# A decoder trunk on one core: scores of the second tile moved behind the retention's outputs, norm rows through the weight queue, an earlier start of ScalarE

## The chip, the cores and the metric

The kernel runs on one core of a Trainium2 chip. The time is that of one launch on the device, in microseconds (us), and every comparison is made with the kernel before on the same chip. The engines are named as in the profile: PE (TensorE, matrix products), DVE (VectorE), ACT (ScalarE), POOL (GpSimd) and SP (SyncE, which only issues transfers here). They run their own instruction streams and meet at semaphores.

## The reference, cut to what matters

256 tokens of width 1024 pass through two layers, all in float32:

```
h += 0.5 * SwiGLU_1(RMSNorm(h))
u  = RMSNorm(h);  z = u @ W_in
h += W_o( sigmoid(gA) * (RWKV7(z_A) @ P_A) + sigmoid(gB) * (Retention(z_B) @ P_B) )
h += CrossAttn_4heads(RMSNorm(h), RMSNorm(mem))
h += 0.5 * SwiGLU_2(RMSNorm(h))
out = RMSNorm(h)                      # after the last layer
```

The retention branch forms scores of query and key tiles (128 tokens each), multiplies them with the values, normalizes each head of 128 columns and multiplies by a row `gn` and a gate:

```
y = _standardize(y, B_GN_EPS).reshape(B, T, B_V_WIDTH) * gn
return y * silu(g)
```

The RWKV-7 branch is a recurrence over tokens; the kernel computes it in two tiles of 128 tokens, in which blocks of triangular systems are inverted.

## The kernel before, in words

Each float32 operand of a product is split into a high part (`wh`, `uh`, ...: rounded, line 241, on ACT) and a low part (`wl`, `ul`, ...: the rest, line 242, on DVE), and three products are formed (high by high, high by low, low by high). Weights come in pieces of 512 KB over SP's queue (line 260) into five raw buffers; the split fills seven pairs of buffers.

PE's order of work is written out by a planner (`Em`, line 77). Each part of the network is a generator that emits its products and then yields a number, the modelled nanoseconds it wants to wait, or an event; the planner takes the ready generator of the best priority. So big projections (`z<-wh,uh` and the like, from `mix`) are interleaved with the chains of the two mixers. PE executes that order strictly. The orders of DVE, ACT, POOL and SP are chosen by a scheduler from dependencies and its own estimates, with the start (line 470) and the ends under a high priority as exceptions; each engine then executes its list strictly too.

PSUM is handed out in eight banks (`s.ps`, a first-in first-out list of free banks), so a product may have to wait until the last reader of its bank is done.

What the change touches:
- `start` (line 470): DVE clears a tile `zero`, PE multiplies it by itself 20 times, ACT makes the first `uh` and `wh`.
- `rw_chain` (line 1124). The products `sc<-beT,alT` give U; its blocks go to HBM (`ug`) and back (`us`), and POOL solves 31 steps, each a product `tm<-xs,us` (line 1162) and a sum `xs<-xs,tm` (line 1167). The result goes out as `xg` (line 1170), comes back as `W` (line 1250), is turned by DVE (`XQ<-W`, line 1254), and PE continues with `iv<-XQ,U`. Ahead of that the generator `late(t)` (line 1180) makes, for each tile t, the scores `sc<-qT,beT` and two groups `sc<-mh,kh` ..., which DVE masks into `S<-sc` (line 1121). The products `R<-zv,S` come from `r_sum(0)`, between `late(0)` and `late(1)`.
- `ret_chain` (line 1410): scores `sc<-bqT,bkT`, masked into `rS`, then four tiles `O<-bv,rS` (24 rows of products in PE's list). For each, ACT squares into `yb`, DVE sums (`bss`), POOL forms the power -1/2 (`brn<-bss,nhalf`, line 265), and DVE multiplies, `yb<-O,brn` (line 1449), which is the last reader of the O bank.
- `ret_g` (line 1398): the gate of the retention; it loads `gn` over POOL's queue and ends in `bg<-bg,rhf,gn` (line 1406) on DVE.
- `acc_last` and `final` (lines 375 and 620): the last additions to h and the final RMSNorm.

Of the kernel before, what the change touches and what calls it, by code (L numbers as in the profile page):

```python
# [10 lines left out]
F32 = mybir.dt.float32  # L11
F32R = mybir.dt.float32r
I32 = mybir.dt.int32
AF = mybir.ActivationFunctionType
ALU = mybir.AluOpType
AX = mybir.AxisListType
P = 128
D = 1024
# [143 lines left out]
class K:  # L162
    NW = 7
    NRAW = 5
    NA = 49
    T_XG, T_W = 57000.0, 6000.0

    def __init__(s, ctx, tc, A):
        s.tc, s.nc, s.A = tc, tc.nc, A
# [71 lines left out]
        s.nc.scalar.activation(hi, src, AF.Copy)  # L241
        s.nc.vector.tensor_tensor(lo, src, hi.bitcast(F32), ALU.subtract)  # L242

    def row(s, ap, name):
        t = s.ar.alloc(name)
        s.nc.gpsimd.dma_start(t, ap.partition_broadcast(P))
        return t

    def load_w(s, view, n, c):
# [18 lines left out]
    def behind(s, ins, other):  # L268

        s.tc.add_manual_dep(ins.ins, other.ins.name, mybir.DependencyInfo(  # L270
            mybir.DependencyClass.NoSync, mybir.DependencyReason.DATA), reason="behind")

    def stats(s, src, n, eps):
        nc = s.nc
        sq = s.ar.alloc("sq0"), s.ar.alloc("sq1")
        ss = s.sm.tile([P, 2], F32, name="ss", tag="ss")
        for i in range(2):
            nc.scalar.activation(sq[i], src[i], AF.Square, accum_out=ss[:, i:i + 1])
        s.ar.free(*sq)
        x = s.sm.tile([P, 1], F32, name="sx", tag="sx")  # L280
        nc.vector.tensor_tensor(x, ss[:, 0:1], ss[:, 1:2], ALU.add)
        nc.vector.tensor_scalar(x, x, 1.0 / n, eps, ALU.mult, ALU.add)
        r = s.sm.tile([P, 1], F32, name="rstd", tag="rstd")
        s.pow_(r, x, 1)
        return r


    def wcols(s, key, dram, c0, c):
# [85 lines left out]

    def acc_last(s, parts, acc, scale):

        ws = [s.W.next(key) for _, key, _ in parts]
        for t in range(2):
            tok = slice(t * P, (t + 1) * P)
            for n in range(2):  # L380
                cs = slice(n * 512, n * 512 + 512)
                for i, (X, key, k) in enumerate(parts):
                    xh, xl = (x[:, tok] for x in X(k))
                    s.mm3(acc[t][n], xh, xl, ws[i][0][:, 0, cs], ws[i][1][:, 0, cs], False, i == len(parts) - 1)
                with s.tc.high_priority():
                    s.nc.vector.scalar_tensor_tensor(s.h[t][n], acc[t][n], scale[t], s.h[t][n], ALU.mult, ALU.add)
                s.ps.free(acc[t][n])
                yield 0
            s.final(t)


    def new_u(s, l, i):
# [77 lines left out]
    def start(s):  # L470

        nc = s.nc
        with s.tc.manual_schedule(engines={nc.vector.engine, nc.scalar.engine}):

            x = s.ar.alloc("zero", F32R, (P, 256))
            nc.vector.memset(x.bitcast(F32), 0.0)
            b = s.ps.alloc("zero")
            for i in range(20):
                nc.tensor.matmul(b[:, 0:256], x[:, 0:P], x, start=i == 0, stop=i == 19)
            s.ps.free(b)  # L480
            s.ar.free(x)
            for j in range(4):
                s.prep_u(2 * j)
                s.prep_u(2 * j + 1)
                s.W.fill(j + 1)
                if j < 3:
                    nc.sync.dma_start(s.hT[:, 2 * j + 2:2 * j + 4, :], s.A["xT"][:, 2 * j + 2:2 * j + 4, :])
            nc.scalar.activation(s.gcol[:, 64:96], s.gcol[:, 64:96], AF.Copy, scale=0.5)
        for j in range(4):
            s.prep_ss(j, 11414.0, 6590.0, nc.gpsimd)  # L490
            s.ev_u[j].t = 0.0
# [125 lines left out]
        for n in range(2):  # L617
            s.nc.gpsimd.dma_start(s.gain[n], s.A["final_norm"][n * 512:(n + 1) * 512].partition_broadcast(P))

    def final(s, t):  # L620
        nc = s.nc
        with s.tc.high_priority():
            r = s.stats(s.h[t], D, 1e-6)
            o = []
            for n in range(2):
                o.append(s.ar.alloc("o"))
                nc.vector.tensor_tensor(o[n], s.h[t][n], s.gain[n], ALU.mult)
            nc.vector.tensor_scalar(o[0], o[0], r, None, ALU.mult)
            nc.scalar.activation(o[1], o[1], AF.Copy, scale=r)
            for n, q in ((0, nc.sync), (1, nc.scalar)):  # L630
                q.dma_start(s.A["out"][0, t * P:(t + 1) * P, n * 512:n * 512 + 512], o[n])
        s.ar.free(*o)


    def setup(s):
        for l in range(DEPTH):
# [79 lines left out]
    def mix(s, l):  # L716
        nc, A = s.nc, s.A
        em = s.em
        X = s.Xu

        def two():
            yield from s.psneed(2)
            return [s.ps.alloc("z"), s.ps.alloc("z")]
# [14 lines left out]
        R = s.R = {"rows": rows}  # L738
# [14 lines left out]
        for nm, q in (("bq", 0), ("bk", 1)):  # L753
            ps = yield from two()
            yield from s.unit(X, nm, 8, 512, ps)
            em.spawn(s.ret_rot(nm, q, ps), 4)
        R["bv"] = [[], []]
        for n in range(2):
            ps = yield from two()
            yield from s.unit(X, "bv", 8, 512, ps)  # L760
            s.ret_v(s.evac(ps, "bv"))
        R["ev_bv"].t = em.now + 4150.0
        em.spawn(s.ret_chain(l), 4)
        R["bg"] = [[], []]
        for n in range(2):
            ps = yield from two()
            yield from s.unit(X, "bg", 8, 512, ps)
            s.ret_g(l, n, ps)
# [52 lines left out]
        acc = [s.ps.alloc("acc") for n in range(4)]  # L821
# [302 lines left out]
    def rw_chain(s, l):  # L1124
# [8 lines left out]
        for t in range(2):  # L1133
# [6 lines left out]
            for k in range(4):  # L1140
                for q in range(2):
# [5 lines left out]
        xs = s.ar.alloc("xs", F32, (P, 16, 32))  # L1147
        tm = s.ar.alloc("tm", F32, (P, 16, 32))
        nc.gpsimd.dma_start(xs, A["x0"])
        nc.gpsimd.tensor_tensor(tm[:, 0:2, 0:29], xs[:, 0:2, 2:3].broadcast_to([P, 2, 29]),  # L1150
                                xs[:, 2:3, 3:32].broadcast_to([P, 2, 29]), ALU.mult)
        for i in range(2):
            for q in range(2):
                nc.sync.dma_start(us[i][q * 64:(q + 1) * 64], ug[:, 16 * i:16 * i + 16, :])
# [18 lines left out]
        t_sol = em.now  # L1173
# [6 lines left out]
        def late(t):  # L1180
            al, q, ka = (T[t][n] for n in ("al", "q", "ka"))
            yield from s.psneed(2)
            yield from s.arneed(2)
            b = s.scores(T[t]["be"], q)
            s.ar.free(T[t]["be"])
            for o in range(2):
                QB[t][o] = s.ar.alloc("S", F32, (P, 4, P))
                s.mask_evac(QB[t][o], b[o], s.masks[:, 1:2, :].broadcast_to([P, 4, P]))
            yield from s.arneed(6)
            kh, kl = (s.ar.alloc(n, F32R, (P, 4, P)) for n in ("kh", "kl"))  # L1190
            s.split(kh, kl, ka)
            s.ar.free(ka)
            mv = [[s.ar.alloc(n, F32R, (P, 2, 2, P)) for n in ("mh", "ml")] for _ in range(2)]
            for i in range(2):
                for c, x in enumerate((al, q)):
                    s.split(mv[i][0][:, :, c, :], mv[i][1][:, :, c, :], x[:, 2 * i:2 * i + 2, :])
            if t == 0:
                s.ar.free(al, q)
            KQ[t][:] = [], []
            for i in range(2):  # L1200
                yield 1776.0
                yield from s.psneed(2)
                yield from s.arneed(2)
                b = [s.ps.alloc("sc") for _ in range(2)]
                for pr in range(2):

                    for n, (x, y) in enumerate(((kh, 0), (kh, 1), (kl, 0))):
                        for o in range(2):
                            p0, p1 = 64 * o, 64 * o + 64
                            s.mm(b[o][:, pr * 256:pr * 256 + 256], x[p0:p1, 2 * i + pr, :],  # L1210
                                 mv[i][y][p0:p1, pr].rearrange("p c t -> p (c t)"), n == 0, n == 2)
                s.em.now -= 650.0
                for o in range(2):
                    x = s.ar.alloc("S", F32, (P, 2, 2, P))
                    s.mask_evac(x, b[o], s.masks.unsqueeze(1).broadcast_to([P, 2, 2, P]))
                    KQ[t][o].append(x)
            s.ar.free(kh, kl, *mv[0], *mv[1])
            yield 5258.0
# [7 lines left out]
        def r_sum(t):  # L1226
            vc = R["v"][t]
            b = s.ps.alloc("R")
            for hd in range(8):
                if t == 1 and hd % 2 == 0:  # L1230
                    s.mm(ps2(b, hd // 2), T[1]["al"][:, hd // 2, :], s.S0[:, hd // 2, :], True, False)
                s.mm(hs(b, hd), kq(t, hd, 0), hs(vc, hd), t == 0, t == 0 or hd % 2 == 1)
            rr = s.ar.alloc("R")
            act.activation(rr, b, AF.Copy)
            s.ps.free(b)
            return rr
# [42 lines left out]

        yield from s.psneed(1)  # L1280
        r0 = r_sum(0)
        yield from late(1)
        yield from inv()
        for t in range(2):
# [112 lines left out]

    def ret_g(s, l, n, ps):
        nc, R = s.nc, s.R
        gn = s.row(s.A["b_gn"][l, n * 512:(n + 1) * 512], "gn")  # L1400
        for t in range(2):
            th = s.ar.alloc("bg")
            nc.scalar.activation(th, ps[t], AF.Tanh, scale=s.rhf[t])
            nc.vector.scalar_tensor_tensor(th, th, 1.0, ps[t], ALU.add, ALU.mult)
            s.ps.free(ps[t])
            nc.vector.scalar_tensor_tensor(th, th, s.rhf[t], gn, ALU.mult, ALU.mult)
            R["bg"][t].append(th)
        s.ar.free(gn)
# [330 lines left out]
```

## Time and profile before

| | us |
|---|---|
| three runs | 1518.89, 1518.98, 1520.46 |
| median | 1518.98 |
| the profiled execution | 1518.1 |
| its span, first to last instruction | 1516.0 |
| PE busy in it | 1495.0 (99%) |
| DVE, ACT, POOL busy | 1061.9, 760.5, 180.7 |
| PE's mean granted clock | 0.992 of full speed |

A row of a timeline gives the start, the duration, the engine, the line, what is written from what, and in brackets how long the engine had stood idle just before and what released it. Rows of one kind that follow one another are drawn together (x16); then the duration is that of the whole group. Products overlap in PE, so the spacing of two starts is what one costs.

### The profile page before, as it was taken

What the parts mean: (1) busy time and instruction counts of PE and PEld (TensorE: products, weight loads), DVE (VectorE), ACT (ScalarE), POOL (GpSimd) and SP (SyncE); (2) the same over time, 40 slices, a digit from 0 to 9 for tenths busy, and PEclk for the clock granted to TensorE, in tenths of its full rate; (3) what the DMA queues carried; (4) which work ended last, traced back from release to release, by engine and by line L of the source; (5) the groups of instructions that cost most, each with busy time, mean ns of one, the idle gap of its engine ahead of it and who ended that gap; (6) DMA issues with size and microseconds to landing.
All of it is one profiled execution on the core that took longest, in us unless ns stands there. A gap on an engine that the chain in (4) does not pass through costs nothing.

```text
span 1516.0 us, 28626 instructions
## 1 busy us (share of the span) xinstructions
PE 1495.0 (99%) x11754; PEld 1417.9 (94%) x11754; DVE 1061.9 (70%) x1463; ACT 760.5 (50%) x1044; POOL 180.7 (12%) x241
## 2 busy tenths in 40 slices
PE   8999999998999999999999999999999999999997
PEld 8999988788999999999999999887889999999996
DVE  7976699967657757655686666899576577665654
ACT  6554465544434656444455445654454446654442
POOL 3210003272000000000001000224700000000000
PEclk9999999999999999999999999999999999999999
DMA  8776655535546545666568665674364455466651
GB/s 303 228 226 195 195 169 189 152 123 181 168 145 190 170 139 183 191 185 188 173 196 244 195 194 156 193 232 138 95 197 157 156 164 191 126 211 184 189 186 41
DMA packets 137546, 270.54 MB, mean 178 GB/s; under 512 B 18804, under 2 KB 29444, under 8 KB 137416
## 3 DMA queue, kind: packets, MB, share of 16 engines
q1 hardware_dynamic: 133960, 259.94, 55.2%
q0 software_dynamic: 3024, 8.19, 1.9%
q8 instruction: 92, 1.51, 0.4%
q10 hardware_dynamic: 432, 0.58, 0.1%
q14 instruction: 38, 0.31, 0.1%
HBM read 263.31 MB, written 2.23 MB: 175 GB/s over the span
## 4 chain that ended last, share of the span: by engine, by line
PE 83%; DVE 6%; POOL 4%; issue 2%; DMA 2%; ACT 1%; SPq 1%; POOLq 0%; DVEq 0%
PE z L207 21%; PE acc L207 21%; PE u L207 16%; PE g L207 16%; PE xq L207 3%; POOL tm L1162 2%; DVE wl L242 2%; POOL xs L1167 1%; PE tp L219 1%; PE Y L207 1%; PE xo L207 1%; PE xs L207 1%; POOL brn L265 1%; PE SA L207 1%; PE sc L207 1%
## 5 line engine op out<-in xcount | busy, mean ns | idle before, releaser
L242 DVE TENSOR_TENSOR wl<-raw,wh 128x1024 fp32r<-128x1024 f32 (+1 forms) x477 | 580.8, 1224 | 312.7 <-ACT wh L241 310.5
L241 ACT ACTIVATE wh<-raw 128x1024 fp32r<-128x1024 f32 (+1 forms) x477 | 501.2, 1057 | 527.6 <-PE z L207 125.6
L207 PE MATMUL g<-uh,wh 128*128 128x256 f32 x704 | 196.9, 280 | 2.0 <-ACT wh L241 2.0
L207 PE MATMUL g<-uh,wl 128*128 128x256 f32 x704 | 196.7, 279 | 0.9 <-DVE wl L242 0.9
L207 PE MATMUL u<-uh,wh 128*128 128x256 f32 x704 | 196.5, 279 | 0.0
L207 PE MATMUL g<-ul,wh 128*128 128x256 f32 x704 | 196.3, 279 | 0.0
L207 PE MATMUL u<-ul,wh 128*128 128x256 f32 x704 | 195.8, 278 | 0.0
L207 PE MATMUL u<-uh,wl 128*128 128x256 f32 x704 | 195.8, 278 | 0.0
L207 PE MATMUL acc<-ah,wh 128*128 128x256 f32 x528 | 146.9, 278 | 0.0
L207 PE MATMUL acc<-al,wh 128*128 128x256 f32 x528 | 146.6, 278 | 0.0
L207 PE MATMUL acc<-ah,wl 128*128 128x256 f32 x528 | 146.6, 278 | 0.0
L207 PEld LDWEIGHTS g<-uh,wh 128*128 128x128 f32 x704 | 132.9, 189 | 2.4 <-ACT wh L241 2.2
L207 PEld LDWEIGHTS g<-uh,wl 128*128 128x128 f32 x704 | 133.0, 189 | 1.3 <-DVE wl L242 1.3
L207 PEld LDWEIGHTS g<-ul,wh 128*128 128x128 f32 x704 | 132.6, 188 | 0.2
L207 PEld LDWEIGHTS u<-uh,wl 128*128 128x128 f32 x704 | 132.3, 188 | 0.0
L207 PEld LDWEIGHTS u<-uh,wh 128*128 128x128 f32 x704 | 132.2, 188 | 0.0
L207 PEld LDWEIGHTS u<-ul,wh 128*128 128x128 f32 x704 | 131.9, 187 | 0.0
L207 PE MATMUL z<-wh,uh 128*128 128x512 f32 (+1 forms) x320 | 126.6, 396 | 0.0
L207 PE MATMUL z<-wh,ul 128*128 128x512 f32 (+1 forms) x320 | 123.2, 385 | 0.4 <-DVE ul L415 0.4
L207 PE MATMUL z<-wl,uh 128*128 128x512 f32 (+1 forms) x320 | 123.3, 385 | 0.0
L207 PEld LDWEIGHTS acc<-ah,wl 128*128 128x128 f32 x528 | 99.2, 188 | 0.0
L207 PEld LDWEIGHTS acc<-ah,wh 128*128 128x128 f32 x528 | 99.1, 188 | 0.0
(404 smaller groups left out, 3311.9 us busy)
## 6 DMA issues: line engine op xcount, KB each, us to landing
raw<-in_ffn_w_in SPq DMA_DIRECT2D x175, 512.0 KB, 4.1
raw<-in_mix_w_in SPq DMA_DIRECT2D x108, 512.0 KB, 4.4
raw<-in_ffn_w_out SPq DMA_DIRECT2D x88, 512.0 KB, 3.5
raw<-in_cross_w_kv SPq DMA_DIRECT2D x32, 512.0 KB, 3.7
raw<-in_w_branch_b SPq DMA_DIRECT2D x16, 512.0 KB, 4.5
raw<-in_mix_w_out SPq DMA_DIRECT2D x16, 512.0 KB, 3.5
raw<-in_cross_w_q SPq DMA_DIRECT2D x16, 512.0 KB, 3.8
raw<-in_cross_w_o SPq DMA_DIRECT2D x16, 512.0 KB, 4.3
```

What stands on the lines that cost most here:

```text
L207: s.nc.tensor.matmul(out, l, r, start=start, stop=stop)
L219: s.nc.tensor.transpose(out, src, s.ident)
L241: s.nc.scalar.activation(hi, src, AF.Copy)
L242: s.nc.vector.tensor_tensor(lo, src, hi.bitcast(F32), ALU.subtract)
L265: i = s.nc.gpsimd.tensor_tensor(out, src, s.nhalf[:, :n], ALU.pow)
L1162: i = nc.gpsimd.tensor_tensor(tm[:, 0:nr, 0:w], xc, row, ALU.mult)
L1167: nc.gpsimd.tensor_tensor(xs[:, 0:nr, k + 1:32], xs[:, 0:nr, k + 1:32], tm[:, 0:nr, 0:w], ALU.add)
```

## The change

Seven edits:
1. ACT reads one column of `zero` right after DVE cleared it, so its table is loaded there and not when hT has landed.
2. 30 products of zeros instead of 20.
3. The rows `gn` are asked for on SP's queue, ahead of the second `bv` unit and of the first `bg` unit, instead of on POOL's queue in `ret_g`.
4. A product on POOL ahead of the solve, whose result nothing read, is gone.
5. `late(1)` waits for the modelled time t_sol + 42 us.
6. T_W, the modelled wait between `W` and `XQ`, is 7500 instead of 6000.
7. The final norm's squares are taken in `acc_last` with the scale 1/32, and the epsilon is added to the first half's sum.

```diff
-    T_XG, T_W = 57000.0, 6000.0
+    T_XG, T_W = 57000.0, 7500.0
...
-    def row(s, ap, name):
+    def row(s, ap, name, q=None):
         t = s.ar.alloc(name)
-        s.nc.gpsimd.dma_start(t, ap.partition_broadcast(P))
+        (q or s.nc.gpsimd).dma_start(t, ap.partition_broadcast(P))
...
+                    sq = s.ar.alloc("sq")
+                    nc.scalar.activation(sq[:, c0:c1], h, AF.Square, scale=1.0 / 32, accum_out=ss[:, e:e + 1])
+                    s.ar.free(sq)
+                    if e == 0:
+                        nc.vector.tensor_scalar(x, ss[:, 0:1], 1e-6, None, ALU.add)
+                    else:
+                        nc.vector.tensor_tensor(x, x, ss[:, e:e + 1], ALU.add)
...
+            nc.scalar.activation(s.sm.tile([P, 1], F32, name="act0", tag="act0"), x[:, 0:1].bitcast(F32), AF.Copy)
             b = s.ps.alloc("zero")
-            for i in range(20):
-                nc.tensor.matmul(b[:, 0:256], x[:, 0:P], x, start=i == 0, stop=i == 19)
+            for i in range(30):
+                nc.tensor.matmul(b[:, 0:256], x[:, 0:P], x, start=i == 0, stop=i == 29)
...
+        R["gn"] = []
+        gn = lambda n: R["gn"].append(s.row(A["b_gn"][l, n * 512:(n + 1) * 512], "gn", nc.sync))
         for n in range(2):
+            if n:
+                gn(0)
             ps = yield from two()
...
         for n in range(2):
+            if n == 0:
+                gn(1)
             ps = yield from two()
...
-        nc.gpsimd.tensor_tensor(tm[:, 0:2, 0:29], xs[:, 0:2, 2:3].broadcast_to([P, 2, 29]),
-                                xs[:, 2:3, 3:32].broadcast_to([P, 2, 29]), ALU.mult)
...
         r0 = r_sum(0)
+        yield max(0.0, t_sol + 42000.0 - em.now)
         yield from late(1)
...
-        gn = s.row(s.A["b_gn"][l, n * 512:(n + 1) * 512], "gn")
+        gn = R["gn"].pop(0)
```

PE's list in the first layer, from the products R on, was this before; the left-out rows are projections `z` and repetitions.

```order
L207 MATMUL R<-zv,S 128x64 x8
L207 MATMUL sc<-qT,beT 128x128 x8
...
L207 MATMUL sc<-mh,kh 128x256 x2
...
L219 MATMUL tp<-ident,ra 128x128 x8
...
L207 MATMUL sc<-bqT,bkT 128x128 x8
...
L207 MATMUL O<-bv,rS 128x128 x24
```

Now it is this. Here the rows carry the tiles' numbers and, in brackets, the engines whose semaphores an instruction waits for; O_3866 and O_3909 are the first and the last of the four O tiles.

```order
L207 MATMUL O_3866<-bv_3416,rS_3770 128x128
...
L207 MATMUL O_3909<-bv_3633,rS_3840 128x128
...
L207 MATMUL sc_3948<-qT_3284,beT_3331 128x128 [waits PE_49]
...
L207 MATMUL sc_4002<-mh_3966,kh_3962 128x256 [waits DVE_49,Activation_49]
L207 MATMUL sc_4003<-mh_3966,kh_3962 128x256 [waits DVE_49,PE_49,Activation_49]
...
L207 MATMUL z_4048<-uh_2337,wh_3701 128x256 [waits DVE_49,Activation_49]
...
L207 MATMUL sc_4056<-mh_3968,kh_3962 128x256 [waits DVE_49]
```

The scores of the second tile (sc_3948 to sc_4057) stand behind the O products. The free list gives sc_4002, sc_4003, z_4048 and z_4049 the four banks of the O tiles, so their waits on DVE are for the four `yb<-O,brn`.

DVE's list in that stretch is now this.

```order
L1449 TENSOR_TENSOR yb_3871<-O_3866,brn_3876 128x512 [waits Pool_49]
...
L1449 TENSOR_TENSOR yb_3888<-O_3879,brn_3893 128x512 [waits Pool_49]
L1449 TENSOR_TENSOR yb_3901<-O_3896,brn_3906 128x512 [waits Pool_49]
...
L1122 TENSOR_TENSOR S_3958<-sc_3948,masks_93 128x512 [waits PE_49]
...
L1449 TENSOR_TENSOR yb_3918<-O_3909,brn_3923 128x512 [waits Pool_49]
```

Each of the four waits for POOL, and the masking of the second tile stands behind three of them.

POOL's list before, from the solve's step 18 (128x10x13) on:

```order
L1167 TENSOR_TENSOR xs<-xs,tm 128x10x13
L246 DMA gn<-in_b_gn 128x512 x2
L1246 MEMSET W 128x512
L265 TENSOR_TENSOR brn<-bss,nhalf 128x4
L1162 TENSOR_TENSOR tm<-xs,us 128x10x12
...
L1167 TENSOR_TENSOR xs<-xs,tm 128x12x9
L265 TENSOR_TENSOR brn<-bss,nhalf 128x4
```

and now:

```order
L1166 TENSOR_TENSOR xs<-xs,tm 128x10x13
...
L1166 TENSOR_TENSOR xs<-xs,tm 128x10x12
L265 TENSOR_TENSOR brn<-bss,nhalf 128x4
L1161 TENSOR_TENSOR tm<-xs,us 128x11x11
...
L1166 TENSOR_TENSOR xs<-xs,tm 128x13x7
L1245 MEMSET W 128x512
L265 TENSOR_TENSOR brn<-bss,nhalf 128x4 x2
```

The two `gn` transfers have left POOL, the first `brn` stands behind step 19 instead of 18, and five steps (20 to 24) and a MEMSET stand between the first and the second `brn`, where four steps stood.

## Rows read from the trace of the kernel before

**Rows 1.** The page's first part: busy time, share of the span and instructions of each engine.

```profile
PE 1495.0 (99%) x11754; PEld 1417.9 (94%) x11754; DVE 1061.9 (70%) x1463; ACT 760.5 (50%) x1044; POOL 180.7 (12%) x241
```

**Rows 2.** The waits of PE over the whole span: what waited, for what, us in total, times, longest.

```profile
PE iv L207 <- DVE XQ L1254: 7.0, 4, 3.2
PE g L207 <- ACT wh L241: 2.0, 1, 2.0
PE sc L207 <- ACT bqT L1045: 1.7, 2, 0.9
```

**Rows 3.** Stretches of the first and then the second layer, PE: from:to, length, PE busy (instructions), granted clock, share of the DMA engines, GB/s.

```profile
362.00:366.00 4.00, 4.00 (x29) 0.50 1.04 394
...
1049.00:1052.00 3.00, 3.00 (x13) 0.50 0.81 196
...
1109.00:1113.00 4.00, 4.00 (x19) 0.50 1.05 404
```

**Rows 4.** PE's timeline around the moved scores and the products `iv`, in the first layer (to 361), and the moved scores in the second.

```profile
301.44 1.16 PE L207 MATMUL sc<-qT,beT 64*128 64x128 f32 x14 [0.87 <-ACT bqT L1045]
...
305.52 0.39 PE L207 MATMUL sc<-mh,kh 64*128 64x256 f32 x2
...
306.43 0.50 PE L207 MATMUL z<-wh,uh 128*128 128x512 f32 x1
...
320.76 5.52 PE L207 MATMUL O<-bv,rS 128*128 128x128 f32 x48
326.04 0.48 PE L207 MATMUL z<-wh,uh 128*128 128x512 f32 x1
...
335.69 0.40 PE L207 MATMUL z<-wh,ul 128*128 128x512 f32 x1
...
359.24 1.05 PE L207 MATMUL iv<-XQ,U 32*32 32x32 f32 x32 [3.16 <-DVE XQ L1254]
...
361.21 1.07 PE L207 MATMUL iv<-XQ,U 32*32 32x32 f32 x32 [0.92 <-DVE XQ L1254]
...
1048.29 1.65 PE L207 MATMUL sc<-qT,beT 64*128 64x128 f32 x14 [0.88 <-ACT bqT L1045]
```

**Rows 5.** POOL's timeline, first layer: the solve, the `gn` transfers and the first two `brn`.

```profile
297.01 8.50 POOL L1162 TENSOR_TENSOR tm<-xs,us 128x58 f32<-128x58 f32 x1
305.59 0.28 POOL L1167 TENSOR_TENSOR xs<-xs,tm 128x58 f32<-128x58 f32 x1
...
324.34 0.42 POOL L1167 TENSOR_TENSOR xs<-xs,tm 128x130 f32<-128x130 f32 x1
324.91 1.11 POOL L246 DMA_DIRECT2D gn<-in_b_gn  x2
...
332.52 1.03 POOL L265 TENSOR_TENSOR brn<-bss,nhalf 128x4 f32<-128x4 f32 x1 [5.96 <-DVE bss L1446]
333.54 0.40 POOL L1162 TENSOR_TENSOR tm<-xs,us 128x120 f32<-128x120 f32 x1
...
337.32 1.02 POOL L265 TENSOR_TENSOR brn<-bss,nhalf 128x4 f32<-128x4 f32 x1
...
349.16 0.26 POOL L1167 TENSOR_TENSOR xs<-xs,tm 128x30 f32<-128x30 f32 x1
349.50 0.59 POOL L1162 TENSOR_TENSOR tm<-xs,us 128x16 f32<-128x16 f32 x1
...
351.57 1.73 POOL L1170 DMA_DIRECT2D xg<-xs  x2 [0.30 <-POOL xs L1167]
```

**Rows 6.** DVE's timeline beside it.

```profile
297.00 0.40 DVE L242 TENSOR_TENSOR ml<-alT,mh 128x256 fp32r<-128x256 f32 x1
...
301.88 3.48 DVE L242 TENSOR_TENSOR wl<-raw,wh 128x1024 fp32r<-128x1024 f32 x3
305.29 1.27 DVE L1121 TENSOR_TENSOR S<-sc,masks 128x512 int32<-128x512 int32 x2
...
328.61 0.75 DVE L1406 SCALAR_TENSOR_TENSOR bg<-bg,rhf,gn 128x512 f32<-128x512 f32 x1 [8.34 <-DMA gn<-in_b_gn]
...
338.38 0.69 DVE L1449 TENSOR_TENSOR yb<-O,brn 128x512 f32<-128x512 f32 x1 [3.31 <-POOL brn L265]
...
349.25 0.75 DVE L1406 SCALAR_TENSOR_TENSOR bg<-bg,rhf,gn 128x512 f32<-128x512 f32 x1
```

**Rows 7.** The start, engines mixed in order of time.

```profile
1.19 4.02 PE L479 MATMUL zero<-zero 128*128 128x256 f32 x20 [1.19 <-DVE zero L476]
...
4.45 1.28 ACT L414 ACT_TABLE_LOAD   x1 [4.45 <-DMA hT<-in_xT]
...
7.23 0.38 PE L207 MATMUL g<-uh,wh 128*128 128x256 f32 x1 [2.02 <-ACT wh L241]
...
9.16 1.06 ACT L241 ACTIVATE wh<-raw 128x1024 fp32r<-128x1024 f32 x1 [0.66 <-DMA raw<-in_ffn_w_in]
...
10.25 1.23 DVE L242 TENSOR_TENSOR wl<-raw,wh 128x1024 fp32r<-128x1024 f32 x1 [0.94 <-ACT wh L241]
...
18.75 0.39 PE L207 MATMUL g<-uh,wl 128*128 128x256 f32 x1 [0.63 <-DVE wl L242]
```

**Rows 8.** The end, DVE.

```profile
1509.96 0.16 DVE L281 TENSOR_TENSOR sx<-ss 128x1 f32<-128x1 f32 x1
1510.15 0.15 DVE L282 TENSOR_SCALAR sx<-sx 128x1 f32<-128x1 f32 x1
```

More of the change, by code (lines that the diff above doesn't have):

```diff
@@ L271, in behind @@
             mybir.DependencyClass.NoSync, mybir.DependencyReason.DATA), reason="behind")
[L273 to L285, printed above, removed]
     def wcols(s, key, dram, c0, c):
@@ L375, in acc_last @@
     def acc_last(s, parts, acc, scale):
+        nc = s.nc
         ws = [s.W.next(key) for _, key, _ in parts]
@@ L379, in acc_last @@
             tok = slice(t * P, (t + 1) * P)
-            for n in range(2):
-                cs = slice(n * 512, n * 512 + 512)
+            o = [s.ar.alloc("o") for n in range(2)]
+            ss = s.sm.tile([P, 2], F32, name="ss", tag="ss")
+            x = s.sm.tile([P, 1], F32, name="sx", tag="sx")
+            ends = (0, 0, 512), (1, 0, 512)
+            for e, (n, c0, c1) in enumerate(ends):
+                cs = slice(n * 512 + c0, n * 512 + c1)
                 for i, (X, key, k) in enumerate(parts):
-                    xh, xl = (x[:, tok] for x in X(k))
-                    s.mm3(acc[t][n], xh, xl, ws[i][0][:, 0, cs], ws[i][1][:, 0, cs], False, i == len(parts) - 1)
+                    xh, xl = (a[:, tok] for a in X(k))
+                    s.mm3(acc[t][n][:, c0:c1], xh, xl, ws[i][0][:, 0, cs], ws[i][1][:, 0, cs], False, i == len(parts) - 1)
                 with s.tc.high_priority():
-                    s.nc.vector.scalar_tensor_tensor(s.h[t][n], acc[t][n], scale[t], s.h[t][n], ALU.mult, ALU.add)
-                s.ps.free(acc[t][n])
-                yield 0
-            s.final(t)
+                    h = s.h[t][n][:, c0:c1]
+                    nc.vector.scalar_tensor_tensor(h, acc[t][n][:, c0:c1], scale[t], h, ALU.mult, ALU.add)
+                    sq = s.ar.alloc("sq")
[5 more added lines that the diff above has]
+                        nc.vector.tensor_tensor(x, x, ss[:, e:e + 1], ALU.add)
+                    nc.vector.tensor_tensor(o[n][:, c0:c1], h, s.gain[n][:, c0:c1], ALU.mult)
+                if c1 == 512:
+                    s.ps.free(acc[t][n])
+                yield 0
+            with s.tc.high_priority():
+                r = s.sm.tile([P, 1], F32, name="rstd", tag="rstd")
+                s.pow_(r, x, 1)
+                nc.vector.tensor_scalar(o[0], o[0], r, None, ALU.mult)
+                nc.scalar.activation(o[1], o[1], AF.Copy, scale=r)
+                for n, q in ((0, nc.sync), (1, nc.scalar)):
+                    q.dma_start(s.A["out"][0, t * P:(t + 1) * P, n * 512:n * 512 + 512], o[n])
+            s.ar.free(*o)
     def new_u(s, l, i):
@@ L618, in h_tok @@
             s.nc.gpsimd.dma_start(s.gain[n], s.A["final_norm"][n * 512:(n + 1) * 512].partition_broadcast(P))
[L620 to L632, printed above, removed]
     def setup(s):
```

## The prediction, made before the changed kernel ran

> **What bounds the kernel now.** First the page's busy line: PE is busy 1495.0 us of a span of 1516.0 [rows 1], so what PE does not wait for costs nothing, and all that can be won is in 21 us of idle time and in stretches at the lower clock. Second the waits of PE, which say where the idle time lies: 7.0 us in four waits of `iv` for XQ, 2.0 for the first `wh`, 1.7 in two waits of the scores `sc<-qT,beT` [rows 2]. Third the windows, since a wait may be followed by the lower of the two clocks: after the `iv` waits the granted clock is 0.50 for 4 us in either layer, and in the second layer for 3 us after the wait of the scores [rows 3]. Work there takes twice as long, so half of such a stretch is lost. Last the timelines of PE, POOL and DVE, which say what a wait ends on [rows 4 to 6].
>
> **What the change can take away.** Scores: they wait 0.87 and 0.88 us [rows 4]. They move behind the O products, some 26 us later, so these two go: 1.75. The clock stretch behind the second (3 us at 0.50) gives 1.5. Waits of `iv`: 3.16 and 0.92 [rows 4], and 7.0 less these, 2.9, in the second layer; the 4 us at 0.50 behind them give 2.0 in either layer. Sum: 1.75 + 1.5 + 7.0 + 4.0 = 14.25, of it 7.0 in the first layer and 7.3 in the second.
>
> **What it adds: PE now waits for POOL.** The four banks of the O tiles go to the second tile's scores and to the first projection behind them. Before, nothing on PE waited for `yb<-O,brn`; now four instructions do, and each `yb` waits for a `brn` that stands in POOL's list between steps of the solve.
>
> When does PE arrive? `z` products start 0.235 apart (326.04 to 335.69 holds 42) and a group of `sc<-mh,kh` takes 0.91 (305.52 to 306.43) [rows 4]. Ahead of O there now stand 66 `z` instead of 48 (+4.2 us), without two such groups (-1.8), the `sc<-qT,beT` (-1.1) and its wait (-0.9): O starts at 320.76 + 0.4 = 321.2 by the first layer's clock. O takes 5.3, six `z` 1.4, `sc<-qT,beT` 1.1, twelve `z` 2.8: PE stands before the first `sc<-mh,kh` at 331.8.
>
> When do the banks come free? POOL is slow there, because DVE stops it: a step's product that needs about 0.3 us took 8.50 from 297.01 on, while DVE ran `ml`, C, g and `wl` one behind the other out of SBUF; it ended when DVE turned to `S<-sc` out of PSUM at 305.29 [rows 5, 6]. Before, DVE had 13.6 us of such instructions up to step 18's end at 324.8: 8.3 in one run (297.00 to 305.29) and 5.3 in three `wl` and two `bv` after it; POOL's rows there are 11.9 us longer than their kind is elsewhere, 8.2 of it in that one. Now DVE's list holds, up to the first `bss`, by the start-to-start times (1.14 to 1.16 a `wl`, half of it an instruction of 512 columns) [rows 6]: a C, two g and four `wl` 6.4, two `bv` 1.2, six more `wl` 6.8, two `bg,gn` 1.3, `kl` 0.6, two `ml` 0.7: 17.0. The 3.4 us more put step 18 at 328.2, or at 327.8 by the share that POOL lost before. Step 19 is ahead of `brn` too: 1.0, and one `wl` on it. So the first `brn` starts between 329.5 and 331; I take 330.3. It takes 1.03 [rows 5], the `yb` 0.69 [rows 6]: 332.0, and PE waits 0.2.
>
> The second `sc<-mh,kh` is the very next instruction, and its bank waits for the second `brn`. Four steps took 3.8 us between the first two before (333.54 to 337.32) [rows 5]; now five steps and a MEMSET of 0.5 are there: 4.9, and DVE's `ml`, `ml` and `yb,bg` out of SBUF stop POOL for about 1.2. Second `brn`: 331.3 + 6.1 = 337.4, ended 338.4; `yb` at 339.1. PE waits 7.2 in all at this place. The third `brn` is right behind, its bank is free before PE comes; the fourth needs a `bss` behind the masking on DVE and two more steps: I put 0.8 on it, between 0 and 1.3. So 8.0 us per layer, and behind such a wait 4 us at 0.50 as behind `iv` [rows 3], another 2.0: 10.0, for both layers 20.0. `iv` itself no longer waits: PE gets there 8 us later than at 359.24 - 3.16 = 356.1, and POOL, whose chain ended in `xg` at 351.57 [rows 5], has little more to do than before.
>
> Bounds. Below: DVE stops POOL no more than before; step 19 then ends at 325.7, the first `brn` waits for `bss` (about 325.2, from O's start and ACT's and DVE's next steps) and ends at 326.7, the second at 332.6, `yb` at 333.3: a wait of 1.5, and no clock loss, as behind the 0.87 in the first layer, where the next stretch ran at full speed. 1.5 per layer. Above: every stop counted in full and `yb,bg` and `bg,gn` hit steps at their start: 340.2 for the second `yb`, 1.3 for the fourth, and a second stretch at 0.50: 8.4 + 1.3 + 3.5 = 13.2 per layer.
>
> One term in that count is worth a look. `bg,gn` on DVE at 349.25 reads two tiles in SBUF; the POOL product of 16 columns that began inside it took 0.59, where one of 30 took 0.26 [rows 5, 6]. The Trainium skill ("SBUF — State Buffer", Who interferes with whom) says that a DVE instruction with two SBUF inputs contends with a GpSimd instruction that reads SBUF, and that the other then fully blocks; the trace agrees as far as that one row goes. By the rule the two `bg,gn`, which now run early since `gn` comes early, stop POOL for 1.3 per layer, as the row has them in the 17.0; if they did not, the sum would be 2.6 us lower.
>
> **The other edits.** `gn` over SP: DVE's 8.34 us of waiting for it [rows 6] goes, but PE does not wait for `bg`; POOL is rid of 1.11 us, at a time when it then waited 5.96 for `bss` anyway [rows 5]. The price is two issues in front of weights, hidden by the raw buffers, and up to 0.4 us on `ug`, so on the solve: within the bounds. The dropped POOL product: POOL waited for `us` there, 0. T_W: 1.44 us of PE work moves in front of `iv`; it would cut its wait, which is already gone, 0.
>
> Start: PE idles 2.02 us for the first `wh`, and ACT loads its table at 4.45, for 1.28 [rows 7]. Now the table is loaded before, and `uh` begins at 4.45 instead of 5.75. Ten more zero products need up to 2.0 at the spacing of the first twenty (4.02) and may end at 7.2, about 1.2 if they speed up as the last did: so `g` starts at 6.0 to 7.2 instead of 7.23. But the third weight lands at 9.16 and its `wl` ends at 11.48 in any case [rows 7], so most of that is waited off there; 0.5 stays, and half of the 0.63 at 18.75: 0.8, between 0 and 2. A new gap before 11.5 could cost clock: -1.5 at worst.
>
> End: one DVE operation less between the last square and the power, 1509.96 to 1510.15 [rows 8]: 0.2.
>
> **Sum.** +20.0 - 14.25 - 0.8 - 0.2 = +4.7. Against the profile's 1518.1 that is 1522.8; the median of the three runs lies 0.9 above that execution: 1523.7.
>
> **Rivals.**
> First: POOL keeps pace. For it: the 13.6 us of stops before were also full of single `wl`, and POOL still got through 19 steps by 324.8. Against: the stops now come one after the other in the very stretch ahead of the first `brn`. At the lower bound: 2 x 1.5 - 14.25 - 1.0 = -12.2; with a wait of 3 us and a clock loss of 1 in each layer, -7.2. Some 1511, between 1506.7 and 1514.
> Second: the new wait takes the place of the old ones at the same price. It decides at a second `yb` near 336.7: 5 us of wait, 2.0 of clock, 7 per layer: 14 - 14.25 - 1.0 = -1.2, 1517.8. For it: the same bounds, whose middle lies there.
> Third, slower by more: the upper bound, two clock stretches per layer, and the gain at the start lost: 26.4 - 14.25 - 0.2 = +12, 1531.
> That the change does what it says without any new wait (PE never starved, all of 14.25 + 1.0 won, 1503.7) would need the second `brn` at 331, which is before POOL can have done 25 steps even without a stop.
>
> **How the numbers follow.** Forecast 0.42, first rival 0.29, second 0.19, third 0.08, no new wait 0.02. About 0.2% (3.0 us) is what a measurement of this kernel can tell from no change: faster means under 1515.9, slower over 1522.0. The forecast spreads over a `yb` at 338.3 to 340, 1521 to 1526.5, a fifth of it within 0.2%: slower 0.42 x 0.8 + 0.08 + 0.05 of the second = 0.46; faster 0.31 and 0.04 of the second = 0.34; same 0.20. The range for 8 in 10 leaves out the third rival and the lower part of the first: 1509 to 1528; the forecast's own is 1521 to 1527.
>
> **What would show it.** In the waits of PE a new row `sc <- DVE yb` (or `z <- DVE yb`) with some 14 to 16 us in two to four waits, the longest near 7, and no row `iv <- DVE XQ`, none of `sc <- ACT bqT`. In POOL's timeline the first `brn` some 30.5 us behind R's last start, with no idle time ahead of it (POOL late, not `bss`). In the windows a stretch at 0.50 right behind that wait in either layer. At the start ACT_TABLE_LOAD near 1.2 us, `uh` at 4.45, a wait of PE for the third `wl` ending near 11.5. At the end a single `sx` behind the last square. I am wrong if POOL has its first `brn` by 328, if that wait is under 4 us, or if `iv` still waits.

## The result and the profile after

The changed kernel takes 1535.91 us (median of four runs, 1535.89 to 1536.43), the kernel before beside it 1519.26: a ratio of 1.0109 [1.0092, 1.0127], 16.7 us slower. The time lies outside the range of the prediction, beyond its upper end of 1528.

The page's first part of the changed kernel:

```profile
PE 1513.1 (99%) x11764; PEld 1438.4 (94%) x11764; DVE 1069.5 (70%) x1463; ACT 761.0 (50%) x1045; POOL 162.0 (11%) x235
```

Its span is 1534.1, so PE idles 21.0 us, just as before [rows 1]. All of the 18.1 us by which the span grew is PE's busy time, in a program with ten more products, all of them zeros. The waits of PE (what waited, for what, us in total, times, longest) answer to [rows 2]:

```profile
PE sc L207 <- DVE yb L1449: 10.4, 2, 5.3
PE g L207 <- DVE wl L242: 2.4, 2, 1.4
```

The waits of `iv` and of `sc<-qT,beT` are gone, and the scores now wait for `yb`, by the path that was foretold. PE's timeline in the first layer (to 343) and the second shows the place:

```profile
332.40 1.16 PE L207 MATMUL sc<-qT,beT 64*128 64x128 f32 x16
...
336.47 0.38 PE L207 MATMUL sc<-mh,kh 64*128 64x256 f32 x1
342.20 0.55 PE L207 MATMUL sc<-mh,kh 64*128 64x256 f32 x1 [5.35 <-DVE yb L1449]
...
1099.64 0.52 PE L207 MATMUL sc<-mh,kh 64*128 64x256 f32 x1 [5.04 <-DVE yb L1449]
```

POOL's timeline in the first layer answers to [rows 5]; there is no idle time ahead of the first `brn`:

```profile
303.14 6.56 POOL L1161 TENSOR_TENSOR tm<-xs,us 128x58 f32<-128x58 f32 x1
...
317.30 0.83 POOL L1166 TENSOR_TENSOR xs<-xs,tm 128x96 f32<-128x96 f32 x1
...
321.46 0.74 POOL L1166 TENSOR_TENSOR xs<-xs,tm 128x126 f32<-128x126 f32 x1
...
331.15 0.42 POOL L1166 TENSOR_TENSOR xs<-xs,tm 128x126 f32<-128x126 f32 x1
...
333.55 1.03 POOL L265 TENSOR_TENSOR brn<-bss,nhalf 128x4 f32<-128x4 f32 x1
...
338.59 0.38 POOL L1166 TENSOR_TENSOR xs<-xs,tm 128x96 f32<-128x96 f32 x1
...
340.30 2.01 POOL L265 TENSOR_TENSOR brn<-bss,nhalf 128x4 f32<-128x4 f32 x2
```

and DVE's timeline beside it:

```profile
309.46 1.27 DVE L983 TENSOR_REDUCE bvm<-bv 128x4 f32<-128x512 f32 x2
...
317.13 0.75 DVE L1406 SCALAR_TENSOR_TENSOR bg<-bg,rhf,gn 128x512 f32<-128x512 f32 x1
...
321.04 0.89 DVE L1406 SCALAR_TENSOR_TENSOR bg<-bg,rhf,gn 128x512 f32<-128x512 f32 x1
...
334.61 0.69 DVE L1449 TENSOR_TENSOR yb<-O,brn 128x512 f32<-128x512 f32 x1 [4.56 <-POOL brn L265]
...
341.36 0.69 DVE L1449 TENSOR_TENSOR yb<-O,brn 128x512 f32<-128x512 f32 x1 [3.07 <-POOL brn L265]
```

So where are the 18 us? Not in a wait. The view that shows them counts products where PE never pauses: stretches of 40 us of FFN work at full clock (from:to, length, busy time with products begun, clock, DMA share, GB/s). First the kernel before:

```profile
60.00:100.00 40.00, 40.00 (x342) 1.00 0.75 232
140.00:180.00 40.00, 40.00 (x355) 1.00 0.62 188
820.00:860.00 40.00, 40.00 (x355) 1.00 0.64 203
```

Then the changed kernel:

```profile
60.00:100.00 40.00, 40.00 (x336) 1.00 0.75 234
140.00:180.00 40.00, 40.00 (x339) 1.00 0.58 184
820.00:860.00 40.00, 40.00 (x340) 1.00 0.70 212
```

PE is "100% busy at clock 1.00" in all six, and yet begins 355 products in one and 339 in another: 40/355 = 112.7 ns a product against 118. The grouped rows show the same as a duration: the down projection was

```profile
L207 PE MATMUL acc<-ah,wh 128*128 128x256 f32 x528 | 146.9, 278 | 0.0
```

before, and is now

```profile
L207 PE MATMUL acc<-ah,wh 128*128 128x256 f32 x528 | 148.6, 282 | 0.0
```

Products overlap, so 4 ns of duration is not yet a cost; the distance between two starts is. Averaged over neighbouring pairs of 256-column products of `g`, `u`, `acc`, `z`, `xq` at full clock (some 8,650 pairs), it is 116.3 ns before and 118.8 after: 2.5 ns x 8,650 = +21.6 us. The 512-column products lie 0.9 ns closer than before (232.4 for 233.3, about 1,220 pairs): -1.1. The ten zero products take 6.58 - 4.02 = +2.6 (below). Against these stand fewer us at the lower clock: 10.2 for 20.4, so -5.1. The sum, +18.0, is the 18.1 of PE's busy time but for 0.1.

The start and the end, engines mixed, answer to [rows 7] and [rows 8]:

```profile
1.18 1.28 ACT L485 ACT_TABLE_LOAD   x1 [1.18 <-PEq L1724]
...
1.19 6.58 PE L488 MATMUL zero<-zero 128*128 128x256 f32 x30 [1.19 <-DVE zero L484]
...
4.64 0.91 ACT L422 ACTIVATE uh<-hT,gcol 128x256 fp32r<-128x256 f32 x2 [1.97 <-DMA gcol<-in_gcol]
...
7.60 0.28 PE L207 MATMUL g<-uh,wh 128*128 128x256 f32 x1
...
12.27 0.39 PE L207 MATMUL g<-uh,wl 128*128 128x256 f32 x1 [1.43 <-DVE wl L242]
...
1528.62 0.16 DVE L385 TENSOR_TENSOR sx<-sx,ss 128x1 f32<-128x1 f32 x1
```

### The profile page after: what moved, and what is told of

Read it like the earlier page. It is cut to its first block, busy times and chain, and to the rows that moved or that the text cites. A ratio compares the mean times of both kernels' runs of the same rounds, so it can differ in the third digit from the quotient of the medians.

```text
span 1534.1 us, 28648 instructions
## 1 busy us (share of the span) xinstructions
PE 1513.1 (99%) x11764; PEld 1438.4 (94%) x11764; DVE 1069.5 (70%) x1463; ACT 761.0 (50%) x1045; POOL 162.0 (11%) x235
```

## The experiments

**What could change a product's spacing?** In these stretches the list of instructions can't: the same products follow one another. But the changed kernel has one tile more. `act0`, the one column that ACT writes to fetch its table, comes from the pool `sm`, which has two buffers of 32 bytes for it in every partition. Pools lie one behind the other in SBUF, and behind `sm` lie `uh` and `ul` (which begin at byte 112,448 of a partition before, 112,512 after) and the 2 KB slots for all else (128,832 and 128,896). The weights, raw and split, lie ahead of it and stay. So the theory: the place of one operand against the other sets the spacing, and 64 bytes cost the time. The rival: the edits themselves, by another order of work or another phase of the three engines.

**b_pad64**: the kernel before, with only the 64 bytes.

```diff
-        ss = s.sm.tile([P, 2], F32, name="ss", tag="ss")
+        ss = s.sm.tile([P, 10], F32, name="ss", tag="ss")
```

> The kernel before, with one small tile (ss) made larger so that uh, ul and the 2 KB slots lie 64 bytes higher, as in the changed kernel; no instruction is changed. Theory A (the place of the operands in SBUF sets the spacing of the products): slower by 14 to 18 us, 1533 to 1537, spacing of g, u, acc products 118.7 to 120 ns. Theory B (the spacing follows from the changed order or start, places do not matter): 1519, within 3 us.

**a_noshift**: the changed kernel with `act0` in a pool of its own behind all others, so that nothing else moves.

```diff
+        s.endp = ep(tc.tile_pool(name="endp", bufs=1))
...
-            nc.scalar.activation(s.sm.tile([P, 1], F32, name="act0", tag="act0"), x[:, 0:1].bitcast(F32), AF.Copy)
+            nc.scalar.activation(s.endp.tile([P, 1], F32, name="act0", tag="act0"), x[:, 0:1].bitcast(F32), AF.Copy)
```

> The changed kernel, with the one-column tile of ScalarE's early instruction in a pool of its own behind all others, so that uh, ul and the slots lie where they lay before; all seven edits stay. Theory A: 1518 to 1522, since in the mixers only 1.2 us were lost between the two traces; spacing 113.3 and 117.8 ns as before. Theory B: 1534 to 1537.

Measured: b_pad64 1539.77, ratio 1.0132 [1.0117, 1.0147]; a_noshift 1515.71, 0.9973 [0.9963, 0.9982]. Eight unused columns, with not one instruction changed, make the kernel before slower by 20.2 us; without the shift the seven edits make it faster by 3.9. The same group in b_pad64 reads

```profile
L207 PE MATMUL acc<-ah,wh 128*128 128x256 f32 x528 | 148.7, 282 | 0.0
```

and in a_noshift

```profile
L208 PE MATMUL acc<-ah,wh 128*128 128x256 f32 x528 | 147.0, 278 | 0.0
```

(lines are one higher there). The mean spacing is 118.9 and 116.4 ns, as the place theory has it; the two times lie 2.8 above and 2.3 below the ranges that I had set for it. The place theory holds, and the rival falls.

**What the edits do without the shift.** PE's waits in a_noshift:

```profile
PE sc L208 <- DVE yb L1450: 9.2, 2, 4.8
PE g L208 <- DVE wl L243: 1.6, 1, 1.6
```

Three kernels take the two edits apart that matter in the mixers. **a_noshift_early** is a_noshift without edit 5:

```diff
-        yield max(0.0, t_sol + 42000.0 - em.now)
```

> As a_noshift, without the wait for t_sol + 42 us: the second tile's scores are back ahead of the O products. Theory A: the waits of iv are back, T_W takes 1.4 us off them per layer, and the waits on yb are gone: 1514 to 1519, a few us under a_noshift if the moved scores cost what the prediction had (+5.7), the same within 2 us if they only swap one wait for another. Theory B: near 1535.

**b_late** is the kernel before with edit 5 alone (the same line added).

> The kernel before with edit 5 alone (the wait for t_sol + 42 us ahead of late(1)). By the prediction's sum +5.7 us, 1525; by its second rival (a new wait at the price of the old ones) within 2 us of 1519. gn still comes over POOL's queue, so DVE waits for it and the first brn comes later, 1 to 3 us more wait on yb than in the changed kernel.

**b_gn_late** is the kernel before with edits 3 and 5 (`gn` over SP's queue, the later scores).

> The kernel before with edits 3 and 5 (gn over SP, the wait ahead of late(1)), nothing else, places as before. If these two are the gain of a_noshift beside start and end: the waits on yb of 9 us in place of scores and iv (8.7) and of two stretches less at the lower clock, some 2 us under the kernel before: 1516 to 1519. T_W is 6000 here, so iv comes 1.4 us earlier on PE; it should still find XQ ready.

Measured: a_noshift_early 1538.55, 1.0122 [1.0107, 1.0137]; b_late 1526.4, 1.0045 [1.003, 1.006]; b_gn_late 1513.51, 0.9962 [0.9947, 0.9977]. The spacing is 116.3 or 116.4 in all three, so these are waits. In a_noshift_early:

```profile
PE O L208 <- DVE rS L1123: 28.2, 2, 14.3
```

Its DVE timeline shows why; ahead of the gate's rows stands `XQ<-W`, which waits for the whole solve:

```profile
347.45 0.45 DVE L1254 STREAM_TRANSPOSE XQ<-W 128x256 f32<-128x256 f32 x1 [17.58 <-DMA W<-xg]
347.82 0.71 DVE L1406 SCALAR_TENSOR_TENSOR bg<-bg,rhf,gn 128x512 f32<-128x512 f32 x1
```

The scheduler puts `XQ` ahead of the last masks `rS` in DVE's strict list, and the O products stand 14 us in each layer. In b_late it is `gn` that DVE stands for:

```profile
321.40 0.75 DVE L1407 SCALAR_TENSOR_TENSOR bg<-bg,rhf,gn 128x512 f32<-128x512 f32 x1 [9.89 <-DMA gn<-in_b_gn]
```

and PE behind it:

```profile
PE sc L207 <- DVE rS L1121: 16.2, 2, 8.2
```

So edit 5 alone costs 6.8 us; the other six without it cost 19.0; edits 3 and 5 together gain 5.9. Neither has a price of its own. b_late comes near the 1525 of the prediction's sum by another wait than the sum's, which is luck, and b_gn_late lies 2.5 below its expected range. Its waits on `yb` (9.5) and half of its time at the lower clock in the mixers (6.8) are only 0.9 less than the 17.2 of before (worked out below); where the rest of the 5.9 (3.5 to 8.0 by its interval) comes from was not found.

**Which way does the place work?** Shift the other way, further, or one operand at a time. **a_pad128** is a_noshift, **b_pad128** the kernel before, both with 128 bytes in front of `uh`, `ul` and the slots; **b_gn_late_pad128** is b_gn_late with the same line.

```diff
-            ss = s.sm.tile([P, 2], F32, name="ss", tag="ss")
+            ss = s.sm.tile([P, 18], F32, name="ss", tag="ss")
```

> a_noshift with uh, ul and the slots 128 bytes higher than before (ss made larger). If the spacing follows the place modulo 128 bytes: 1516, spacing 113.3 and 117.8. If any move away from the place of before costs: 1533 to 1538. A third spacing is possible: then the time is neither.

> The kernel before with ss made larger so that uh, ul and the slots lie 128 bytes higher; no instruction changed. If the place alone gave a_pad128 its spacing of 113.3 ns: 1494 to 1500 (1519.4 less 22.6, what a_pad128 has against a_noshift). If the spacing at that place is a state that depends on what ran before, not on the place: anything from 1494 to 1519, with stretches at 117.8.

> b_pad128 with edits 3 and 5. If the spacing is that of the place: 1490 to 1494, 4 to 7 us under b_pad128 (b_gn_late had 5.9 under the kernel before), and within 3 us of a_pad128, so that edits 1, 2, 4, 6 and 7 are worth no more than that.

Measured: a_pad128 1493.16, 0.983 [0.9815, 0.9844]; b_pad128 1501.09, 0.9879 [0.9863, 0.9896]; b_gn_late_pad128 1494.21, 0.9833 [0.9818, 0.9847]. The mean spacing is 114.0 or 114.1 in all three, and the 512-column products lie at 230.0 to 230.2 for 233.3. In b_pad128 each of the three stretches now reads as the faster ones of before did:

```profile
60.00:100.00 40.00, 40.00 (x355) 1.00 0.75 239
140.00:180.00 40.00, 40.00 (x355) 1.00 0.65 197
820.00:860.00 40.00, 40.00 (x355) 1.00 0.65 193
```

In b_pad128 PE reaches the old waits sooner, and they grow:

```profile
PE iv L207 <- DVE XQ L1254: 8.8, 4, 3.7
PE sc L207 <- ACT bqT L1045: 4.2, 2, 2.4
```

a_pad128, with 1493.16, beats the kernel before by 26 us and the changed one by 43. At this place the seven edits are worth 8 us (26.3 less 18.2 gained against the kernel before), of it edits 3 and 5 some 7.

**One operand at a time.** **a_slots64** and **a_slots128** are the changed kernel with `act0` between `ul` and the slots, so that the slots alone move, by 64 or 128 bytes (columns 16 or 32):

```diff
+        s.endp = ep(tc.tile_pool(name="endp", bufs=1))
         s.ar = Slots(ep(tc.tile_pool(name="ar", bufs=1)), s.NA, "a", (P, 512))
...
+            nc.scalar.activation(s.endp.tile([P, 16], F32, name="act0", tag="act0")[:, 0:1], x[:, 0:1].bitcast(F32), AF.Copy)
```

**a_all64** and **a_all128** take `act0` from `const`, ahead of the weights, so that weights, `uh`, `ul` and slots move together:

```diff
+            nc.scalar.activation(s.const.tile([P, 16], F32, name="act0")[:, 0:1], x[:, 0:1].bitcast(F32), AF.Copy)
```

> The changed kernel, with ScalarE's one-column tile in a pool between uh, ul and the 2 KB slots: only the slots lie 64 bytes higher, uh and ul where they lay before. If each product's spacing follows its own moving operand: g and u (uh, ul) at 113.3 and 117.8 ns, acc (ah, al in slots) at 118.7 to 120; acc is 528 x 3 products of some 8,600, so 4 to 6 us above the 1515.7 of a_noshift. If the uh and ul alone matter: 1516. If the slots set it for all: 1534 to 1538.

> The changed kernel, with ScalarE's one-column tile made 64 bytes and put among the constants: raw and split weights move by 64 bytes together with uh, ul and the slots. If the distance between weights and moving operand sets the spacing: 1516 as a_noshift. If the absolute place of uh, ul and slots does: 1534 to 1538 as the changed kernel.

> The changed kernel with ScalarE's tile made 128 bytes and put among the constants: weights, uh, ul and slots all lie 128 bytes higher, so their distances are those of a_noshift. If the distance between weights and moving operand alone sets the spacing: 1516, with 113.3 and 117.8. If the absolute place of the moving operand does: 1493, 113.3 nearly throughout.

> The changed kernel with ScalarE's tile made 128 bytes and put between ul and the slots: only the slots lie 128 bytes higher than before, uh and ul are not moved. If each product follows its own moving operand: acc at 113.3 and g, u at 113.3 and 117.8 as in a_noshift, about 1508 to 1512. If the slots decide for all: 1493. If uh and ul do: 1516.

| kernel | moved, bytes | median, us | ratio | spacing g, u / acc, ns |
|---|---|---|---|---|
| a_noshift | none | 1515.71 | 0.9973 [0.9963, 0.9982] | 116.2 / 115.9 |
| the changed kernel | uh, ul, slots 64 | 1535.91 | 1.0109 [1.0092, 1.0127] | 118.9 / 118.8 |
| a_slots64 | slots 64 | 1529.99 | 1.0068 [1.0053, 1.0083] | 117.8 / 118.6 |
| a_slots128 | slots 128 | 1521.62 | 1.0016 [1.0006, 1.0025] | 117.8 / 116.9 |
| a_all64 | all 64 | 1524.13 | 1.0031 [1.0018, 1.0044] | 117.5 mean of all |
| a_all128 | all 128 | 1523.49 | 1.0025 [1.0014, 1.0036] | 117.4 mean of all |
| a_pad128 | uh, ul, slots 128 | 1493.16 | 0.983 [0.9815, 0.9844] | 113.7 / 114.0 |

None of the four new times is one that I had expected. The table rules out that the absolute place of `uh` and the slots alone decides: a_all128 has `uh` and the slots at the bytes of a_pad128 and is 30 us slower. Wherever an operand lies 64 bytes further from its weights, its products are the slowest: all of them in the changed kernel, `acc` alone in a_slots64, whose `g` and `u` keep 117.8. With the old distance (a_all64, a_all128) the 118.7 to 120.0 of the changed kernel is gone. So distance has a part in it. It is not all: the two long stretches at 113.3 of before (from about 110 to 195 us and from 780 to 945) are gone in these two kernels, though short ones near 570 and 1310 us stay, and `g` and `u` stand at 117.8 nearly throughout in both slots kernels, where their operands lie as before; and `acc` in a_slots128 has the distance that it has in a_pad128, but 116.9 for 114.0. What else a kernel needs for the fastest level these runs don't show.

**Is it the phase?** Two kernels with 20 zero products instead of 30 start PE's stream at another moment: **a_pad128_z20** and **a_noshift_z20**.

```diff
-            for i in range(30):
+            for i in range(20):
```

> a_pad128 with 20 zero products instead of 30 (edit 2 undone). If the place sets the spacing: within 2 us of 1493, the start 0 to 1 us earlier or later. If the spacing is a state set by what ran before: stretches at 117.8 may come, up to 1515.

> a_noshift with 20 zero products. By the place: within 2 us of 1515.7 and the same stretches at 113.3 and 117.8. By a state set at the start: other stretches, 1495 to 1523.

Measured: 1494.05, 0.9833 [0.9818, 0.9847], and 1514.28, 0.9963 [0.9948, 0.9978], with spacings of 114.0 and 116.2: as with 30. So ten zero products more or fewer make no difference to the time that can be told.

But the place alone doesn't fix where the faster stretches lie. a_noshift and a_noshift_early have every buffer at the same bytes, and their engines begin the same instructions in the same order for the first 290 us. In a_noshift the first stretches read

```profile
60.00:100.00 40.00, 40.00 (x354) 1.00 0.78 243
140.00:180.00 40.00, 40.00 (x342) 1.00 0.61 185
```

and in a_noshift_early the other way round:

```profile
60.00:100.00 40.00, 40.00 (x342) 1.00 0.75 231
140.00:180.00 40.00, 40.00 (x355) 1.00 0.61 190
```

a_noshift_z20 has 342 and 355 there, like the kernel before. So something in the timing of an execution takes part, which no run here holds fixed; the stretches near 570, from 780 to 945 and near 1310 us come at the same work in all four, as near as the 10 us slices of the traces tell.

## Why the prediction was wrong, and where it was right

**The step that failed** is the first: "what PE does not wait for costs nothing, and all that can be won is in 21 us of idle time and in stretches at the lower clock". It takes a product's cost as fixed. The kernel spaces its 256-column products at two levels, 113.3 and 117.8 ns, at one clock, and that could be seen: 342 products in one full stretch, 355 in another. A third level came with the change. So a term was missing, and edit 1 was costed for its time on ACT alone, when its dearest part is the place that its column takes: +20.2 us alone (b_pad64 against before) and +20.2 among the seven edits (the changed kernel against a_noshift). The sum had nothing for this.

**The new wait: mechanism right, size wrong.** That PE waits for POOL by way of `yb<-O,brn` at the second `sc<-mh,kh`, once a layer, with POOL late and not `bss`, came as said, also that `iv` and the first scores stop waiting. The term was 7.2 + 0.8 and 2.0 of clock per layer. I size it on a_noshift, where products cost what they did. PE begins the first `sc<-mh,kh` at 332.43, against 331.8 predicted; a_noshift runs 1.3 us late there (its first R product starts at 299.56, in the kernel before at 298.26), so PE comes at 331.1 on the prediction's clock, early by 0.7. POOL is early by far more. The second `brn` starts at 335.70, or 334.4 without the 1.3, against 337.4:

```profile
304.90 0.29 POOL L1162 TENSOR_TENSOR tm<-xs,us 128x58 f32<-128x58 f32 x1
...
328.95 1.03 POOL L266 TENSOR_TENSOR brn<-bss,nhalf 128x4 f32<-128x4 f32 x1
...
335.70 2.01 POOL L266 TENSOR_TENSOR brn<-bss,nhalf 128x4 f32<-128x4 f32 x2
```

The first is early by 2.7 (328.95 - 1.3 against 330.3). At 327.7 it also falls under the prediction's own sign of being wrong, a first `brn` by 328. So the mis-sized term is the "17.0" us of DVE's instructions in the way of POOL, turned into 3.0 to 3.4 us of delay: step 18 ends at 327.98, or 326.7 without the 1.3, 1.9 later than before (324.8), and step 19 behind it takes 1.0 with no `wl` on it, where I had put one. POOL was stopped less. In the changed kernel the long stop took 6.56 us and ended when DVE turned to an instruction with one input (309.46), as it had ended before when DVE turned to one with an input in PSUM. The wait was 4.8 and 4.4 in a_noshift, 5.35 and 5.04 in the changed kernel, and the 0.8 for `z` never came.

**The clock behind a wait** was right in kind: the granted clock falls to 0.50, the level of 1.2 GHz, behind the wait in either layer of the changed kernel (from:to, length, busy time, clock, ...):

```profile
338.00:341.00 3.00, 0.00 (x0) 1.00 0.00 0
342.00:348.00 6.00, 5.80 (x25) 0.50 0.01 3
349.00:353.00 4.00, 4.00 (x37) 1.00 0.67 179
...
1100.00:1103.00 3.00, 3.00 (x15) 0.50 0.02 5
```

The size was off on both sides. I had read such stretches from windows of 4 and 3 us that were wholly at 0.50. Before, the two behind `iv` are longer:

```profile
359.50:366.00 6.50, 5.58 (x78) 0.50 0.88 286
...
1107.00:1113.00 6.00, 5.13 (x51) 0.50 0.94 317
```

From end to end those in the mixers before are 6.8, 3.4 and 6.8 us long, 17.0 in all for the 11 of the sum, so what goes is 8.5 and not 5.5. What comes is 6.8 and 3.4 in the changed kernel (10.2, so 5.1), and 6.8 twice in a_noshift.

**So the swap was about even.** Before: waits 7.0 + 1.7 and 8.5 of clock, 17.2. a_noshift: 9.2 + 6.8 = 16.0. The changed kernel: 10.4 + 5.1 = 15.5. The predicted 20.0 - 14.25 = +5.75 is -1.2 or -1.7. That is the second rival, "the new wait takes the place of the old ones at the same price", which had 14 - 14.25 = -0.25 for the swap and decided at a second `yb` near 336.7: in a_noshift it ends at 337.46, or 336.2 without the 1.3. With the column behind all pools 1515.71 came out, between the first rival (1511) and the second (1517.8); these terms leave a part of its gain of 3.9 unexplained.

**The place of the rule.** The Trainium skill ("SBUF — State Buffer", Who interferes with whom) says that a DVE instruction with two SBUF inputs contends with a GpSimd instruction that reads SBUF. The trace of the changed kernel agrees: beside the two `bg,gn` POOL's sums took 0.83 and 0.74, where their like took 0.38 and 0.42 elsewhere. That is 0.8 us, not the 1.3 that I put into the 17.0.

**The other edits.** The end has a single `sx`, as said; the stretch from the last product's start to the end of the span is 0.5 us shorter (7.2 for 7.7), for 0.2 predicted. The table is loaded at 1.18 and `uh` starts at 4.64, for 4.45 as said. But the 30 zeros end only at 7.77, 0.22 apiece, slower than the slower pace that I had bounded them by, and the first `g` starts at 7.60, later than before; PE then waits for the third `wl` to 12.27. The gain of 0.8 did not come. In a_noshift the first `g` starts at 6.63, but then PE works at 0.50 for 3.4 us, and the first FFN ends 1.3 later. This is the cost in the clock that I had named as the worst at the start.

## What to carry to other kernels

Before costing an edit that adds, drops or resizes a tile, list which buffers move with it, and by how much against their partners in a product; a column that nobody reads can cost more than every wait in the kernel. When PE is 99% busy, count products per us in stretches at full clock: two counts for the same work mean there is something to be won that no wait shows, and a pad of 64 or 128 bytes in front of a pool is a quick thing to try. Two edits that share an engine's strict list have no prices of their own, so try them together and apart.

## What the hardware did that I had not expected

Products of 256 columns with the same operands, in the same order and at clock 1.00 came at 113.3, 117.8 or 118.7 to 120.0 ns, and which of these a kernel saw, and for how long, changed with where the moving and the stationary operand lay in SBUF. 64 bytes more between `uh`, `ul`, slots and the weights cost 20 us of 1519; 128 bytes gained 18.2 (b_pad128 against before) or 22.6 (a_pad128 against a_noshift). At one and the same place the kernel before changes between 113.3 and 117.8 within an execution; its stretches at 113.3 last some 30 to 160 us. b_pad128 isn't at 113.3 throughout either: from 550 to 570 us it begins 173 products in 20 us, where the kernel before has 179 from 560 to 580. Why a kernel changes level was not found, nor what in the SBUF makes the difference. Only shifts of 64 and 128 bytes were tried, and they don't show whether there is a better one.
